# Output projection: a second set of accumulators in idle PSUM tiles, partial sums stored from ScalarE's queue, t3 loaded in place

## The chip, the cores and the metric

The kernel runs on one core of one Trainium2 chip. The metric is the device time of one execution in microseconds (us); less is better.

## The reference

A two-layer backbone works on 1024 latent tokens of 1024 channels, in float32. The first layer is a convolution branch beside a gated linear recurrence, the second a pooling mixer. What matters here is the end of the second layer, its output projection, the gated residual and the final norm:

```python
def odd_mixer(h, p, on_grid):
    ...
    y = jnp.einsum("bngi,gij->bngj", d, p["w_grp"]).reshape(bn, n, W_POOL) * p["scale"]
    return (y * jax.nn.silu(g)) @ p["w_out"]      # (1024 x 2048) @ (2048 x 1024)
...
        x = x + gate[:, None] * out_x
    return rmsnorm(x, final_g)
```

## The kernel before

Channels lie on the 128 partitions and tokens along the free dimension, so the projection has a weight of 2048 x 1024, an input `y` of 16 tiles of 128 x 1024 and an output of 8 such tiles. The 2048 input channels are taken in two **parts** of 1024. Part 0's result, times the gate and added to `x`, goes to DRAM (`x1_part`); part 1 reads it back (`x2_load`), adds its own, and the final norm follows.

**Blocks.** Within a part the output is made in four blocks: block `m` (0, 2, 4, 6) is the output tiles `m` and `m+1`, each in two halves of 512 tokens. A block is a two-by-two matrix product done with seven half-size products instead of eight. The seven operands made from `y` are named `b11, t1, t2, b21, t3, b22, t4`; the weights have seven matching combinations, here weight 1 to weight 7. Each operand and each weight is split into a high half of reduced precision (`fp32r`, by a cast on ScalarE, ACT) and a low half (the rest, by a subtraction on VectorE, DVE; both in `split`, lines 97 to 99). A product (`prod`, lines 1148 to 1157) runs over four steps of 128 input channels with three matmuls each: high x high (L1152), high weight x low operand (L1154), low weight x high operand (L1155). So it is 12 matmuls of 128 x 512, and its third matmul is the first that needs the weight's low half.

**Accumulators.** A block uses three PSUM tiles of one bank, `a`, `c` and `b`. `a` takes b11, is copied by ACT into `b` (`evac`), and goes on with b21; `c` takes t1 and b22; `b` takes t2, t3 and t4 on top of the copy. In between, `put` takes partial values out: `keep_part` copies one with ACT (L1209), `copied` does so for the second half (L1836), L1898 adds them on DVE, and `gated` (L1828) multiplies by the gate and adds the sum to a tile `xp` that has been loaded from `x1_part` (L1892) and is then stored there (L1901). The three PSUM tiles come from the pool `pm`, which has four buffers, so a block's tiles are those that the block before has just used. The other four banks are the tiles `c0` and `c1` (one bank each) and the two-bank tile `xb` of the pool `pc`; in this stage they are idle until the final norm.

**Order on PE.** The matmuls of the projection are chained by hand (`linked`). For part 0, block `m` runs b11 and t1, then t4 of the block before (`pend`, `last`), then t2, b21, and t3 and b22 in the order given. Blocks 0 and 2 of part 1 are written out with the class `Quad`; blocks 4 and 6 follow in `last_half0` and in the tail.

**Weights.** `wquad_steps` loads the two raw tiles of a block (`wr`, two buffers, L1116) on SyncE's (SP's) DMA queue and makes the seven weights from them. L1132 is `s3`, from which weight 7 is made; L1133 makes the raw of weight 5, L1134 that of weight 6, L1141 that of weight 3. The order of making is 1, 5, 6, 2, 7, 3, 4. The next block's raw tiles can be loaded when the last split of this block has read them.

**Operands.** The operands of `y` have been stored in DRAM (`y_raw`); `y_operand` loads an operand in two halves (L1703) and splits each. With `raw_tile` given, the load goes into a tile of its own; without, it goes "in place" into the tile that later holds the low half. `y_sums` (L1096 to L1100) makes t1 to t4 for two tiles of `y`; for the last two tiles it is called in the middle of part 0's block 2. Its tile `yt` is a `vtile`, of which there are two buffers; they are shared with every second `xp` tile. The `xp` tiles take turns between `vtile` and `atile`, two buffers each.

**Order on the other engines.** It is planned when the kernel is built, from the priorities, the dependences and modelled times. `issue_after` (and `held`) keeps an instruction behind another, and `high_priority` lets the `put`s and copies go ahead. Each engine, SP's queue among them, then runs its list in order: an instruction that waits holds those behind it.

Of the kernel before, what the change touches and what calls it, by code (L numbers as in the profile page):

```python
# [20 lines left out]
KT = D // P  # L21
H = 512
HALF = (slice(0, H), slice(H, S))
# [24 lines left out]
BOPS = ("b11", "t1", "t2", "b21", "t3", "b22", "t4")  # L48
# [3 lines left out]
def body(ctx, tc, xT, ctxT, cc, ccol, modT, modW, win, gw, wout, wu, grp, wg, wo1, small, edge, ident, outT):  # L52
    nc = tc.nc
# [15 lines left out]
    x1_part = [dram.tile([P, S], F32, tag=f"x1_part{j}", name=f"x1_part{j}") for j in range(KT)]  # L69
# [13 lines left out]
    def psum(name):  # L83
        return pm.tile([P, H], F32, tag="mm", name=name)


    def wide(name):
        return pc.tile([P, S], F32, tag="xb", name=name)


    def banks(name, n):
        if n % 2:
            t = wide(name)
            return [t[:, h] for h in HALF]
        return [pc.tile([P, H], F32, tag=f"c{i}", name=f"{name}_{i}") for i in range(2)]

    def split(src, hi, lo, eng):
        return (nc.scalar.copy(hi, src),  # L98
                eng.tensor_tensor(out=lo, in0=src, in1=hi.bitcast(F32), op=sub))

    def held(after):
        return tc.issue_after(after.ins) if after is not None else nullcontext()

    def split_held(src, hi, lo, eng, low):
        nc.scalar.copy(hi, src)
        with held(low):
            eng.tensor_tensor(out=lo, in0=src, in1=hi.bitcast(F32), op=sub)

    class Written:

        def __init__(self, eng):
            self.eng, self.last = eng, None
# [184 lines left out]
    with ExitStack() as sctx:  # L297
# [335 lines left out]
        for i in range(2):  # L633
            v = cx[i].rearrange("p (k n) -> p k n", n=C)
# [185 lines left out]
    with ExitStack() as actx:  # L820
# [79 lines left out]
        w = w_vg0  # L900
# [202 lines left out]
    loaded, parted, subbed = [None], [], [None]  # L1103


    def wquad(*args, **kw):
        ops = {}
        for _ in wquad_steps(ops, *args, **kw):
            pass
        return tuple(ops[n] for n in range(1, 8))  # L1110

    def wquad_steps(ops, src, name, ring, late=False, hold=None):
# [98 lines left out]
    kept_ = [None]  # L1211
# [483 lines left out]
    def y_operand(ops, part, name, raw_tile, alloc, later=None, hold=None):  # L1695
        hi, lo = [], []
        for q in range(2):
            if raw_tile is None:
                lo.append(alloc(f"y{part}_{name}l{q}", F32R))
                r = lo[q].bitcast(F32)  # L1700
            else:
                r = raw_tile(f"yr_{part}_{name}_{q}")
            d = nc.sync.dma_start(r, y_raw[part][name][:, q * S : (q + 1) * S])  # L1703
            if name in ("b22", "t4"):
                y_loaded[name == "t4"] = d
            hi.append(alloc(f"y{part}_{name}h{q}", F32R))
            if raw_tile is not None:
                lo.append(alloc(f"y{part}_{name}l{q}", F32R))
            if later is not None:
                later.append((r, hi[q], lo[q]))  # L1710
            else:
                with held(hold):
                    split(r, hi[q], lo[q], nc.vector)
        halves = lambda ts: [t[:, h] for t in ts for h in HALF]
        ops[name] = halves(hi), halves(lo)
# [3 lines left out]
    def y_operands(part, raws, names=BOPS, alloc=None, later=None, hold=None):  # L1719
        for name in names:  # L1720
            y_operand(yops[part], part, name, next(raws),
                      alloc or (dtile if name in ("b11", "b21", "t4") else d2tile), later, hold)
# [8 lines left out]
            return wpool.tile([P, D], F32R, tag=tag, name=name)  # L1731
        return ring

    def wo1_weights(part, m):
        return wquad([wo1[m + i, part] for i in range(2)], f"wo{part}_{m}", wo1_ring,
                     part == 1 and m >= KT - 4)

    wo1_ring = wo_ring(iter(["x", "x", "x", "wh", "wl", "wh", "wl"] + ["wh", "wl", "d", "d"] * 14))
    vps, silu = [], [None]
# [94 lines left out]
    def copied(name, x):  # L1834
        t = ttile(f"b_{name}")
        copied_[0] = nc.scalar.copy(t, x)  # L1836
        return t

    copied_ = [None]

    chain = [None]

# [2 lines left out]
            chain[0] = prod(*args)  # L1845
        return chain[0]

    def quad_linked(w, name, ops, put, ahead, order, pend):
        p1, p2, p3, p4, p5, p6, p7 = w
        a, c, b = psum(f"qa_{name}"), psum(f"qc_{name}"), psum(f"qb_{name}")  # L1850
        linked(a, p1, ops["b11"], True, False)
        with tc.high_priority(offset=EVAC):
            evac = nc.scalar.copy(b, a)
        linked(c, p5, ops["t1"], True, False)
        with tc.high_priority(offset=EVAC):
            put(1, 1, c, 0)
        if pend is not None:
            pend()
        linked(b, p6, ops["t2"], False, False)
        with tc.high_priority(offset=EVAC):  # L1860
            put(0, 1, b, 0)
        linked(a, p2, ops["b21"], False, True)
        with tc.high_priority(offset=EVAC):
            put(0, 0, a, None)
        with tc.issue_after(evac.ins):
            nxt_ = ahead()
        for name in order:
            if name == "t3":
                linked(b, p7, ops["t3"], False, False)
                with tc.high_priority(offset=EVAC):  # L1870
                    put(1, 1, b, 1)
            else:
                linked(c, p3, ops["b22"], False, True)
                with tc.high_priority(offset=EVAC):
                    put(0, 1, c, 1)

        def last():
            linked(b, p4, ops["t4"], False, True)
            with tc.high_priority(offset=EVAC):
                put(1, 0, b, None)  # L1880
        return nxt_, last

    last_ = None
    for m in range(0, KT, 2):

        def put(i, h, x, part, m=m, parts={}):
            if part == 0:
                keep_part(parts, f"wo0_{m}", i, x)
                return
            xp_n[0] += 1  # L1890
            t = (vtile, lambda name: atile(name)[:, :H])[xp_n[0] % 2](f"xp{m}_{i}_{h}")
            nc.sync.dma_start(t, x1_part[m + i][:, HALF[h]])  # L1892
            if part == 1:

                if i == 1:
                    x = copied(f"wo0_{m}", x)
                s = x if i == 0 else parts[i]
                nc.vector.tensor_tensor(out=s, in0=x, in1=parts[i], op=add)  # L1898
                x = s
            gated(m + i, t, x)  # L1900
            nc.sync.dma_start(x1_part[m + i][:, HALF[h]], t)  # L1901
            if (m, i, h, part) == (2, 1, 1, 1):
                y_sums(NK - 2)
        def nxt(m=m):
            if m == 0:
                with tc.issue_after(kept_[0].ins):
                    for v in y_late:
                        split(*v, nc.vector)
            if m < KT - 2:
                with tc.issue_after(stored[0].ins):  # L1910
                    return wo1_weights(0, m + 2)
            w = wo1_weights(1, 0)
            y_operands(1, iter([xtile]), BOPS[3:4])
            return w

        if m == KT - 2:
            with tc.issue_after(loaded[0].ins):
                y_operands(1, iter([xtile] * 2), BOPS[1:3])
        w, last_ = quad_linked(w, f"wo0_{m}", yops[0], put, nxt, ("b22", "t3") if m else ("t3", "b22"), last_)
        if m == 2:  # L1920
            with tc.issue_after(loaded[0].ins):
                y_operands(1, iter([xtile]), BOPS[:1], lambda name, dt: xtile(name, dt), hold=copied_[0])
# [8 lines left out]
    def wo1_put(m):  # L1931
        def put(i, h, x, part):
            v = x1[m + i][:, HALF[h]]
            if i == 1 and part == 1:
                x = copied(f"wo1_{m}", x)
            gated(m + i, v, x)
            if part != 0:
                square_fin(m + i, h, slice(0, H), v)
        return put

    class Quad:

        def __init__(self, w, name, put):
            self.w, self.name, self.put = dict(zip(range(1, 8), w)), name, put
            self.ps = {}

        def bank(self, n):
            if n not in self.ps:
                self.ps[n] = psum(f"q{n}_{self.name}")
            return self.ps[n]  # L1950

        def run(self, op):
# [12 lines left out]
            with tc.high_priority(offset=EVAC):  # L1965
                self.evac = nc.scalar.copy(self.bank("b"), self.bank("a"))

    q0 = Quad(w, "wo1_0", wo1_put(0))
    for n in "acb":
        q0.bank(n)  # L1970
    q0.run("b11")
    q0.copy()
    q0.run("t1")
    last_()
    q0.run("t2")
    q0.run("b21")
    with tc.issue_after(q0.evac.ins):
        late_ = []
        y_operands(1, iter([None]), BOPS[5:6])
        y_operands(1, iter([xtile]), BOPS[4:5])  # L1980
        with held(y_loaded[0]):
            y_operands(1, iter([None]), BOPS[6:], later=late_)
        w = wo1_weights(1, 2)
        for v in late_:
            split(*v, nc.vector)
        with held(y_loaded[1]):
            x2_load(2)
    q2 = Quad(w, "wo1_2", wo1_put(2))
    q2.run("b11")
    q0.run("t3")  # L1990
    q0.run("b22")
# [300 lines left out]
```

## Time and profile before

| | us |
|---|---|
| median of three runs | 1278.67 |
| lowest and highest of them | 1275.99, 1279.72 |
| the profiled execution | 1275.34 |
| its span (first to last instruction) | 1273.5 |
| its granted TensorE clock, mean | 0.995 |

A row of a timeline gives the start, the length in us, the engine, the line of the kernel, the operation, the tiles (output <- inputs, buffer numbers left out), and in square brackets how long the engine stood idle before it and what ended that. Rows of neighbouring equal instructions are merged (x2, x3). A row of waits gives who waited, for whom, the total in us, how often, and the longest. `wq_wo` are the split weights of this projection, `wr_wo` the raw ones, `y_t4l` is the low half of operand t4 and `y_t4h` its high half, `qa_wo`, `qb_wo` and `qc_wo` are the accumulators, `b_wo` and `s_wo` the copies out of them. `wo0_2` is block 2 of part 0, `wo1_0` block 0 of part 1.

### The profile page before, as it was taken

The numbers are of one execution on the slowest core, as the hardware profiler recorded it, in microseconds if no ns is written. First come the engines' busy times: TensorE is split into PE (matmuls) and PEld (weight loads), VectorE is DVE, ScalarE is ACT, GpSimd is POOL, SyncE is SP. The second block draws the span as 40 slices with busy tenths as digits, with TensorE's granted clock in tenths as the row PEclk, the third lists the DMA queues.
The fourth block names the chain that finished last, engine by engine and source line by source line (L and its number), as shares of the span: only waits on it lengthen the run. The fifth ranks groups of instructions, "written<-read, shape, count | busy, mean of one in ns | idle before, by whom it ended". The sixth has DMA issues, their size and how long they took to land. (4 is left out here: it accounts for less than half of the span.)

```text
span 1273.5 us, 16213 instructions
## 1 busy us (share of the span) xinstructions
PE 1254.7 (99%) x5858; PEld 1036.0 (81%) x5858; DVE 1139.2 (89%) x1748; ACT 655.9 (51%) x955; POOL 295.0 (23%) x176
## 2 busy tenths in 40 slices
PE   9999999999999999999999999999999999999996
PEld 7788888888888888888887888888888888777785
DVE  7799999999999999989888979999999977878876
ACT  8464566556656533237444446644444444735542
POOL 0015364436443557434210032000000000000003
PEclk9999999999999999999999999999999999999998
DMA  9970111112111234432526665334333235868713
GB/s 375 380 254 33 58 59 58 50 47 70 59 66 58 75 116 142 157 131 83 175 90 232 201 225 159 105 139 157 124 116 100 107 116 182 279 193 268 284 67 133
DMA packets 78705, 182.29 MB, mean 143 GB/s; under 512 B 7712, under 2 KB 23328, under 8 KB 78624
## 3 DMA queue, kind: packets, MB, share of 16 engines
q1 hardware_dynamic: 69632, 176.53, 40.7%
q10 hardware_dynamic: 8992, 4.72, 1.3%
q8 instruction: 46, 0.75, 0.3%
q14 instruction: 35, 0.29, 0.1%
HBM read 137.18 MB, written 44.04 MB: 142 GB/s over the span
## 5 line engine op out<-in xcount | busy, mean ns | idle before, releaser
L670 DVE SCALAR_TENSOR_TENSOR conv<-u,sm,conv 128x505 f32<-128x505 f32 (+6 forms) x224 | 153.8, 747 | 1.0
L2012 POOL TENSOR_TENSOR o<-x,rr 128x256 f32<-128x256 f32 (+1 forms) x10 | 9.8, 1012 | 455.6 <-ACT rr L2012 455.6
L670 ACT ACTIVATE l<-g,sm 128x512 f32<-128x512 f32 (+1 forms) x96 | 58.7, 619 | 57.7 <-PE g L670 57.0
L670 POOL TENSOR_TENSOR l<-l,l 128x1280 f32<-128x1280 f32 x16 | 47.1, 2966 | 25.6 <-ACT l L670 15.1
L670 PE MATMUL gb<-h0h,wl_gb 128*128 128x512 f32 x128 | 49.9, 390 | 0.4 <-POOL wl_gb L670 0.4
L670 PE MATMUL va<-h0h,wl_va 128*128 128x512 f32 x128 | 49.9, 390 | 0.2 <-DVE wl_va L670 0.2
L670 PE MATMUL gb<-h0h,wh_gb 128*128 128x512 f32 x128 | 49.9, 389 | 0.0
L670 PE MATMUL gb<-h0l,wh_gb 128*128 128x512 f32 x128 | 49.8, 389 | 0.0
L670 PE MATMUL va<-h0l,wh_va 128*128 128x512 f32 x128 | 49.8, 389 | 0.0
L670 PE MATMUL va<-h0h,wh_va 128*128 128x512 f32 x128 | 49.8, 389 | 0.0
L670 PE MATMUL wob<-ybh,wh_wob 128*128 128x512 f32 x128 | 49.8, 389 | 0.0
L670 PE MATMUL wob<-ybl,wh_wob 128*128 128x512 f32 x128 | 49.8, 389 | 0.0
L670 PE MATMUL wob<-ybh,wl_wob 128*128 128x512 f32 x128 | 49.8, 389 | 0.0
L670 DVE TENSOR_TENSOR_SCAN l<-l,l 128x256 f32<-128x256 f32 (+1 forms) x32 | 48.7, 1521 | 1.1
L670 DVE SCALAR_TENSOR_TENSOR conv<-cL,wsum,conv 128x506 f32<-128x506 f32 (+3 forms) x70 | 48.2, 746 | 0.2
L670 POOL TENSOR_TENSOR l<-l,uc 128x1280 f32<-128x1280 f32 x16 | 47.7, 3008 | 0.0
L98 ACT CAST wq_g<-wr_g 128x512 fp32r<-128x512 f32 x48 | 28.2, 620 | 31.7 <-DMA wr_g<-wg 12.2
L670 PE MATMUL xb<-h0l,wh_xb 128*128 128x512 f32 x112 | 43.8, 391 | 0.0
L670 PE MATMUL xb<-h0h,wh_xb 128*128 128x512 f32 x112 | 43.8, 391 | 0.0
L670 PE MATMUL xb<-h0h,wl_xb 128*128 128x512 f32 x112 | 43.6, 389 | 0.0
L670 PE MATMUL vg<-h0h,wh_vg 128*128 128x512 f32 x112 | 43.6, 389 | 0.0
L670 PE MATMUL vg<-h0l,wh_vg 128*128 128x512 f32 x112 | 43.6, 389 | 0.0
(624 smaller groups left out, 4312.4 us busy)
## 6 DMA issues: line engine op xcount, KB each, us to landing
modw<-modW SPq DMA_DIRECT2D x16, 512.0 KB, 10.7
x_part<-xp SPq DMA_DIRECT2D x32, 256.0 KB, 2.4
mod<-modT SPq DMA_DIRECT2D x32, 256.0 KB, 3.7
wr_v<-wfold SPq DMA_DIRECT2D x16, 512.0 KB, 3.9
wr_g<-wg SPq DMA_DIRECT2D x16, 512.0 KB, 4.4
wr_wo<-wo SPq DMA_DIRECT2D x16, 512.0 KB, 4.6
mod<-modT SPq DMA_DIRECT2D x14, 512.0 KB, 4.2
yr_t<-y_t SPq DMA_DIRECT2D x14, 512.0 KB, 6.5
```

The lines of the kernel that those rows point to most:

```text
L98: return (nc.scalar.copy(hi, src), eng.tensor_tensor(out=lo, in0=src, in1=hi.bitcast(F32), op=sub))
L670: last[eng] = f(*args, **kw)
L2012: tail[eng] = f(*args, **kw)
```

## The change

1. In part 0, blocks 2 and 6 (`m % 4 == 2`) take `a` and `c` from the tiles `c0` and `c1` and `b` from the second half of `xb` (`spare`). Block 2 of part 1 (`q2`) does so too. The other blocks stay in `pm`.
2. The stores of part 0's sums to `x1_part` are no longer issued on SP right behind `gated`. They are kept in a list (`kept_out`) and issued on ACT's DMA queue (`stores`), held behind a later copy: behind `copied` of the same block (all but the newest when it isn't the first block), behind the `keep_part` copy of t1 of the next block, and at the end behind the copy `q0.evac` of part 1's first block.
3. In part 0's block 0, the splits of t4 are taken out of the list that runs ahead of the next block's weights; they are issued after weight 5, through the new argument `mid` of `wquad`, and their subtractions are held behind weight 5's low half.
4. In part 1, t3 is loaded in place and first; the raw weights of block 2 are held behind its second load; b22 and t4 are loaded in place behind those raw weights, and both are split behind the weights' splits. Before, the order was b22 (in place), t3 (through a tile of its own), t4 (in place), weights.

```diff
-    def wquad(*args, **kw):
+    def wquad(*args, mid=None, **kw):
         ops = {}
         for _ in wquad_steps(ops, *args, **kw):
-            pass
+            if mid is not None:
+                mid()
         return tuple(ops[n] for n in range(1, 8))
...
-            if name in ("b22", "t4"):
+            if name in ("t3", "t4"):
                 y_loaded[name == "t4"] = d
...
-    copied_ = [None]
+    copied_, kept_out = [None], []
+
+    def stores(after, n):
+        with held(after):
+            for _ in range(n):
+                nc.scalar.dma_start(*kept_out.pop(0))
...
+    def spare(name):
+        a, c = banks(f"qac_{name}", 0)
+        return a, c, wide(f"qb_{name}")[:, HALF[1]]
+
-    def quad_linked(w, name, ops, put, ahead, order, pend):
+    def quad_linked(w, name, ops, put, ahead, order, pend, other):
         p1, p2, p3, p4, p5, p6, p7 = w
-        a, c, b = psum(f"qa_{name}"), psum(f"qc_{name}"), psum(f"qb_{name}")
+        a, c, b = spare(name) if other else [psum(f"q{n}_{name}") for n in "acb"]
...
         with tc.high_priority(offset=EVAC):
             put(1, 1, c, 0)
+            stores(kept_[0], len(kept_out))
         if pend is not None:
             pend()
...
+    def second_late():
+        with tc.issue_after(kept_[0].ins):
+            for v in y_late[2:]:
+                split_held(*v, nc.vector, parted[1])
...
                 if i == 1:
                     x = copied(f"wo0_{m}", x)
+                    stores(copied_[0], len(kept_out) - (m > 0))
...
             gated(m + i, t, x)
-            nc.sync.dma_start(x1_part[m + i][:, HALF[h]], t)
+            kept_out.append((x1_part[m + i][:, HALF[h]], t))
...
             if m == 0:
                 with tc.issue_after(kept_[0].ins):
-                    for v in y_late:
+                    for v in y_late[:2]:
                         split(*v, nc.vector)
+                with tc.issue_after(stored[0].ins):
+                    return wo1_weights(0, 2, second_late)
...
-        w, last_ = quad_linked(w, f"wo0_{m}", yops[0], put, nxt, ("b22", "t3") if m else ("t3", "b22"), last_)
+        w, last_ = quad_linked(w, f"wo0_{m}", yops[0], put, nxt, ("b22", "t3") if m else ("t3", "b22"), last_,
+                               m % 4 == 2)
...
     q0.run("t1")
+    stores(q0.evac, 2)
     last_()
     q0.run("t2")
+    stores(q0.evac, 1)
     q0.run("b21")
     with tc.issue_after(q0.evac.ins):
         late_ = []
-        y_operands(1, iter([None]), BOPS[5:6])
-        y_operands(1, iter([xtile]), BOPS[4:5])
+        y_operands(1, iter([None]), BOPS[4:5])
         with held(y_loaded[0]):
-            y_operands(1, iter([None]), BOPS[6:], later=late_)
-        w = wo1_weights(1, 2)
+            w = wo1_weights(1, 2)
+        with tc.issue_after(loaded[0].ins):
+            y_operands(1, iter([None] * 2), BOPS[5:], later=late_)
         for v in late_:
             split(*v, nc.vector)
         with held(y_loaded[1]):
             x2_load(2)
-    q2 = Quad(w, "wo1_2", wo1_put(2))
+    q2 = Quad(w, "wo1_2", wo1_put(2), spare("wo1_2"))
```

More of the change, by code (lines that the diff above doesn't have):

```diff
@@ L1732, in wo_ring, with wo1_weights @@
         return ring
-    def wo1_weights(part, m):
+    def wo1_weights(part, m, mid=None):
         return wquad([wo1[m + i, part] for i in range(2)], f"wo{part}_{m}", wo1_ring,
-                     part == 1 and m >= KT - 4)
+                     part == 1 and m >= KT - 4, mid=mid)
     wo1_ring = wo_ring(iter(["x", "x", "x", "wh", "wl", "wh", "wl"] + ["wh", "wl", "d", "d"] * 14))
@@ L1941, in body, with __init__ @@
     class Quad:
-        def __init__(self, w, name, put):
-            self.w, self.name, self.put = dict(zip(range(1, 8), w)), name, put
-            self.ps = {}
+        def __init__(self, w, name, put, tiles):
+            self.w, self.put = dict(zip(range(1, 8), w)), put
+            self.ps = dict(zip("acb", tiles))
         def bank(self, n):
-            if n not in self.ps:
-                self.ps[n] = psum(f"q{n}_{self.name}")
             return self.ps[n]
@@ L1966, in copy @@
                 self.evac = nc.scalar.copy(self.bank("b"), self.bank("a"))
-    q0 = Quad(w, "wo1_0", wo1_put(0))
-    for n in "acb":
-        q0.bank(n)
+    q0 = Quad(w, "wo1_0", wo1_put(0), [psum(f"q{n}_wo1_0") for n in "acb"])
     q0.run("b11")
```

## The prediction

> **What bounds the kernel now.** I read the page's busy times first, then the waits of PE behind 900 us, then the busy times by stretch, then PE's timeline, and last the timelines of DVE, ACT and SP around each hole.
>
> ```profile
> PE 1254.7 (99%) x5858; PEld 1036.0 (81%) x5858; DVE 1139.2 (89%) x1748; ACT 655.9 (51%) x955; POOL 295.0 (23%) x176
> ```
> ```profile
> PE qc_wo L1152 <- DVE xp L1828: 2.8, 2, 1.8
> PE qa_wo L1155 <- DVE wq_wo L99: 1.9, 2, 1.2
> ...
> PE qa_wo L1152 <- ACT wq_wo L98: 0.4, 1, 0.4
> ...
> PE qb_wo L1154 <- DVE y_t3l L99: 0.2, 1, 0.2
> ```
> ```profile
> 1093.50:1217.00 123.50, 118.14 (x506) 95.10 (x505) 99.74 (x141) 65.58 (x101) 0.00 (x0) 0.99 0.70 236
> 1110.00:1130.00 20.00, 16.93 (x66) 12.97 (x66) 12.04 (x19) 6.16 (x12) 0.00 (x0) 0.91 0.38 126
> ...
> 1170.00:1190.00 20.00, 20.00 (x89) 16.33 (x87) 15.61 (x23) 8.26 (x13) 0.00 (x0) 1.00 0.88 312
> ```
>
> PE is the bound, and the stage that the diff touches, 1093.5 to 1217 us, still has holes in it. Columns of the last view are start:end, length, PE, PEld, DVE, ACT, POOL, granted clock, DMA share, GB/s. DVE is busy 99.74 of 123.5 us there: a shorter stage leaves it less slack.
>
> ```profile
> 1093.51 0.39 PE L1152 MATMUL qa_wo<-y_b11h,wq_wo 128*128 128x512 f32 x1
> ...
> 1109.83 0.39 PE L1152 MATMUL qc_wo<-y_b22h,wq_wo 128*128 128x512 f32 x1
> ...
> 1114.46 0.50 PE L1155 MATMUL qa_wo<-y_b11h,wq_wo 128*128 128x512 f32 x1 [1.25 <-DVE wq_wo L99]
> ...
> 1118.88 0.47 PE L1152 MATMUL qc_wo<-y_t1h,wq_wo 128*128 128x512 f32 x1 [1.82 <-DVE xp L1828]
> 1119.19 0.40 PE L1154 MATMUL qc_wo<-y_t1l,wq_wo 128*128 128x512 f32 x1
> 1119.43 0.46 PE L1155 MATMUL qc_wo<-y_t1h,wq_wo 128*128 128x512 f32 x1
> ...
> 1120.33 0.63 PE L1155 MATMUL qc_wo<-y_t1h,wq_wo 128*128 128x512 f32 x1
> ...
> 1123.32 0.45 PE L1152 MATMUL qb_wo<-y_t4h,wq_wo 128*128 128x512 f32 x1
> ...
> 1159.91 0.47 PE L1152 MATMUL qc_wo<-y_t1h,wq_wo 128*128 128x512 f32 x1 [0.95 <-DVE xp L1828]
> ...
> 1190.49 0.50 PE L1152 MATMUL qa_wo<-y_b11h,wq_wo 128*128 128x512 f32 x1 [0.38 <-ACT wq_wo L98]
> ...
> 1191.84 0.50 PE L1155 MATMUL qa_wo<-y_b11h,wq_wo 128*128 128x512 f32 x1 [0.61 <-DVE wq_wo L99]
> ...
> 1194.83 0.50 PE L1154 MATMUL qb_wo<-y_t3l,wq_wo 128*128 128x512 f32 x1 [0.21 <-DVE y_t3l L99]
> ...
> 1216.94 0.39 PE L1152 MATMUL qa_l<-y_b11h,wq_wo 128*128 128x512 f32 x1
> ```
>
> The first two rows are six products of 12 matmuls apart: 16.32 us over 72, a cadence of 0.2267 us. The first and the last row are 42 products apart (one left over from before, four blocks of seven, wo1_0's seven, six of wo1_2's): 504 matmuls, 114.2 us at that cadence, against 123.4 measured. So 9.2 us are lost in the stage, and that is the ceiling of the gain. The six named waits are 5.2 of it. Between 1120.33 and 1123.32 seven starts take 2.99 us instead of 1.59: 1.4 us at a low clock (granted 0.91 over that stretch). The other 2.6 us are restarts, about 0.3 us behind each wait (first matmuls of 0.50 instead of 0.39), and crumbs.
>
> **Part by part.** *The two bank waits (1118.88 and 1159.91).* Both wait for a `gated` of the block before on its c accumulator. With wo0_2, wo0_6 and wo1_2 in the other three tiles, neither bank has a reader when it is wanted. At 1159.91 nothing else is late, so 0.95 plus a restart goes: 1.2 us. At 1118.88 something is just behind it:
>
> ```profile
> 1111.97 0.69 DVE L1132 TENSOR_TENSOR ws_wo<-wr_wo,wr_wo 128x512 f32<-128x512 f32 x1 [0.81 <-DMA wr_wo<-wo]
> 1112.58 1.22 DVE L99 TENSOR_TENSOR y_t4l<-yr_t,y_t4h 128x1024 fp32r<-128x1024 f32 x1
> 1113.72 0.68 DVE L99 TENSOR_TENSOR wq_wo<-wr_wo,wq_wo 128x512 fp32r<-128x512 f32 x1
> ...
> 1114.92 0.68 DVE L1133 TENSOR_TENSOR wr_wo<-wr_wo 128x512 f32<-128x512 f32 x1
> ...
> 1117.99 0.75 DVE L1828 SCALAR_TENSOR_TENSOR xp<-qc_wo,m,xp 128x512 f32<-128x512 f32 x1
> 1118.65 1.89 DVE L99 TENSOR_TENSOR wq_wo<-wr_wo,wq_wo 128x512 fp32r<-128x512 f32 x3
> ```
> ```profile
> 1115.64 0.62 ACT L98 CAST wq_wo<-wr_wo 128x512 fp32r<-128x512 f32 x1 [2.20 <-DVE wr_wo L1133]
> ```
>
> The bank came free at 1118.74; the low half of weight 5, first of the three in 1.89 us from 1118.65, was ready about 1119.3, and the third matmul of t1 (1119.43) needs it. With the bank free and nothing else changed PE would stop two matmuls later. The edit `second_late` matters here: it takes the y_t4l subtraction (1112.58) from ahead of weight 1's low half and holds it behind weight 5's. Everything after it moves up 1.14 us, the distance of the two starts.
>
> *Weight 1 (1114.46).* Its low half then starts at 1112.58 and ends near 1113.25; the third matmul was due at 1113.0. Left 0.3 and a restart: 1.0 of 1.5 saved.
>
> *Weight 5.* Due near 1116.0 then. In today's order it would be ready about 1118.2, 2.1 us late. L1133 no longer stands behind y_t4l; right behind weight 1's low half, or one or two `gated` operations later, it starts at 1113.2 to 1114.4, and cast and subtraction (0.62, 0.69) put weight 5 at 1115.3 to 1116.5. I take 0.5 late and a restart: 1.5 of 2.3 saved. y_t4l's two subtractions (2.4 us) then run from 1116.5 to 1118.9; t4's product comes two products and the two rests of waiting behind b11's 1112.6, near 1119.4, so they are covered with half a microsecond to spare. Without that cover they would cost what they overrun.
>
> *The clock.* The 1.4 us follow two waits of 1.25 and 1.82 us within 6 us; the waits of 0.95, and of 0.38, 0.61 and 0.21 together, are followed by none. With waits of 0.3 and 0.5 I count it gone: 1.4 saved, bounds 0 and 1.4. The Trainium skill (TensorE: Matmul & The Clock Gate, Part 1) has the clock halve after at least one idle window of about 3.4 us; no hole here is that long, so by that rule these waits did not cause the drop, it would stay, and the sum would be 1.4 smaller. The trace speaks for a finer trigger; it is a rival below.
>
> *t3 in place, weights earlier (wo1_2).*
>
> ```profile
> 1188.87 1.05 ACT L98 CAST y_b22h<-y_b22l 128x1024 fp32r<-128x1024 f32 x1 [4.30 <-DMA y_b22l<-y_b]
> 1189.83 1.13 ACT L98 CAST wq_wo<-wr_wo 128x512 fp32r<-128x512 f32 x2
> ```
> ```profile
> 1177.75 1.54 SPq L1116 DMA_DIRECT2D wr_wo<-wo  x2
> ```
>
> ACT stood 4.30 us at the cast of y_b22h, with weight 1's cast behind it although its rows had come: the subtraction of L1132, which needs both raw tiles, ran at 1187.65. The diff sends t3 first, then the weights, then b22 and t4, whose splits come behind the weights'. The blocking cast goes, and t3, needed by the next product, is there: 0.9 us (0.21, an unnamed second hole at its other half, two restarts). Its first load goes into tiles that wo0_6's t3 product reads, as b22's second load (1179) did, so SP stands until that product is done, and the weights' loads stand behind it. And 1 MB of t3 now stands ahead of the weights on SP where 0.5 MB of b22 stood, on DMA engines 0.88 busy at 312 GB/s: 0.5 MB is 1.6 us. So of 1.5 us (0.38, 0.61, two restarts) I save 1.0.
>
> *The stores.*
>
> ```profile
> L1901 SPq DMA_DIRECT2D x_part<-xp x16: 319/320/628, 1110.1 to 1189.0; - x16
> ...
> DMA to landing us min/median/max: 2.0/4.1/9.4
> ```
> ```profile
> L285 ACTq DMA_DIRECT2D wfold<-fo x16: 366/366/385, 750.1 to 795.0; - x16
> ```
>
> Sixteen issues leave SP (5.1 us) and cost ACT 5.9 us at 0.366; ACT is busy 65.58 of 123.5 us, so I cost them at nothing, with SP's loads freed from waiting behind a `gated`. Uncovered, each would be 0.4. They add waits on ACT: each stands there until its `gated` has run on DVE, and the casts and the copies b<-a that PE wants stand behind it. By the order of the calls the sums stored behind a copy are those of the products before it, already gated when the copy runs; the exceptions are the last two groups, behind q0's copy, where ACT stood idle for 4.30 us in the row above. Bounds 0 and 2 us, taken 0. The Trainium skill (DMA: Bandwidth & Descriptors, Issuing engines are not separate DMA queues) says that issuing from several engines saves only sequencer time; by that rule too the bytes gain nothing. What the holding-back costs is tiles, the slower rival.
>
> *Sum.* 1.2 + 1.0 + 1.5 + 1.4 + 0.9 + 1.0 = 7.0. PE then asks 4 to 6 us sooner for raws that go round by DMA and DVE; bounds 0 and 3, from the 0.88 DMA share and DVE's 24 us of slack; I take 1.0. Gain 6.0 us: the profiled execution goes from 1275.34 (span 1273.5 and 1.84 around it) to 1269.3. The median of the runs, 1278.67, lies 3.33 above it: **1272.7**.
>
> **Rivals.**
> *Weight 5 takes the bank's place.* The planner keeps DVE's order of today; t1 stops 2.1 us and the clock drops again. Weight 5's 1.5 and the 1.4 are not saved: gain 3.1, 1275.6. For it: the 1118.65 row; against: program order puts weight 5 ahead of weights 6, 2 and 7.
> *The low clock stays.* Gain 4.6, 1274.1.
> *DVE stands at a held-back tile (slower).*
>
> ```profile
> 1129.82 0.70 DVE L1096 TENSOR_TENSOR yt<-y,y 128x512 f32<-128x512 f32 x1 [2.77 <-DMA x_part<-xp]
> ```
> ```profile
> 1139.94 0.57 ACT L1836 COPY b_wo<-qb_wo 128x512 f32<-128x512 f32 x1
> ```
>
> The tile of `yt` is that of wo0_0's last sum, and DVE waited 2.77 us for its store already. That store now goes behind the copy of wo0_2 (1139.94): 0.57 + 0.37 + 9.4 at the longest landing is 1150.3, and the four sums end near 1152.8. If they stand ahead of weight 6's low half, wanted by t2's product at 1145.2, PE stops 7.6 us, with a restart and, for a hole over twice as long, twice the clock's 1.4: 10.7 lost against 6.0 saved, 1283.4. It turns to a loss if landing passes about 5 us and the planner puts the sums ahead. Against it: the median landing is 4.1, and DVE may take the sums later.
> *It does nothing:* the waits return at other weights, 1278.7.
>
> **How the numbers follow.** A measurement here can tell about 0.3% (3.8 us; the three runs span 3.7). Forecast 0.48, weight 5 0.22, DVE stands 0.17, clock stays 0.08, nothing 0.05. Faster by over 0.3% (under 1274.8): 0.48 + 0.06 + 0.06 of weight 5 = 0.60; same 0.23 (0.16 of weight 5, the rest from nothing and the edges); slower 0.17. Range: full removal of 9.2 with a fast set of runs, 1268.5 (0.03 below), up to 1280.5, which leaves out the stand of DVE. The likeliest case alone: 1269.5 to 1274.7.
>
> **What would show it.** Right: no PE wait on `xp` L1828 in this stage, no row near 0.63 us, granted clock 1.00 in the stretch behind 1110, under 3.5 us lost of 114.2. Weight 5: a wait of t1 on DVE `wq_wo`. DVE stands: a long idle before L1096, PE waiting on `wq_wo` in wo0_4. I am wrong if the stage is not shorter than 120 us, or if the loss returns behind 1217 us.

## The result, and the profile after

The median fell from 1276.84 us (six runs, 1275.99 to 1279.72; the 1278.67 of the start were the first three such runs) to **1269.06 us** (six runs, 1267.5 to 1270.9): a ratio of 0.9935 [0.992, 0.995], 7.8 us between the medians. The profiled executions stand at 1275.34 and 1268.66, their spans at 1273.5 and 1266.9. Lines of the kernel behind 1106 have moved: the raw loads, L1116, are L1117 now, L1152, L1154 and L1155 of before are L1153, L1155 and L1156 now, L1132 to L1134 are L1133 to L1135, L1828 is L1829, and the stores, L1901 on SP before, are L1845 on ACT.

The page's busy times, PE's waits in the stage, and the same stretches as before (start:end, length, PE, PEld, DVE, ACT, POOL, granted clock, DMA share, GB/s), of the changed kernel:

```profile
PE 1251.0 (99%) x5858; PEld 1034.7 (82%) x5858; DVE 1140.9 (90%) x1748; ACT 655.1 (52%) x955; POOL 295.0 (23%) x176
```
```profile
PE qac_wo L1156 <- DVE wq_wo L99: 1.2, 2, 0.8
...
PE qc_wo L1155 <- DVE y_b22l L99: 0.4, 1, 0.4
PE qac_wo L1153 <- ACT wq_wo L98: 0.3, 1, 0.3
```
```profile
1093.00:1210.50 117.50, 115.52 (x506) 94.32 (x506) 99.20 (x141) 65.18 (x101) 0.00 (x0) 1.00 0.70 248
...
1110.00:1130.00 20.00, 19.23 (x86) 15.59 (x85) 13.89 (x20) 7.66 (x13) 0.00 (x0) 1.00 0.47 154
...
1170.00:1190.00 20.00, 20.00 (x89) 16.54 (x89) 19.96 (x29) 11.96 (x17) 0.00 (x0) 1.00 0.94 345
```

The same 506 matmuls and 141 DVE instructions stand in 117.5 us instead of 123.5. The 20 us behind 1110 hold 86 matmuls where there were 66, at a granted clock of 1.00 instead of 0.91. PE's waits sum to 1.9 us where they were 5.2, and none is on `xp`, that is, on a bank. PE's timeline, shortened to the ends of the stage and all of its waits, says where they are:

```profile
1093.04 0.39 PE L1153 MATMUL qa_wo<-y_b11h,wq_wo 128*128 128x512 f32 x1
...
1116.22 0.50 PE L1156 MATMUL qac_wo<-y_t1h,wq_wo 128*128 128x512 f32 x1 [0.77 <-DVE wq_wo L99]
...
1154.43 0.50 PE L1153 MATMUL qac_wo<-y_t1h,wq_wo 128*128 128x512 f32 x1 [0.29 <-ACT wq_wo L98]
...
1155.64 0.50 PE L1156 MATMUL qac_wo<-y_t1h,wq_wo 128*128 128x512 f32 x1 [0.48 <-DVE wq_wo L99]
...
1192.87 0.50 PE L1155 MATMUL qc_wo<-y_b22l,wq_wo 128*128 128x512 f32 x1 [0.44 <-DVE y_b22l L99]
...
1210.46 0.39 PE L1153 MATMUL qa_l<-y_b11h,wq_wo 128*128 128x512 f32 x1
```

From first to last row 117.42 us; against 114.2 for the 504 matmuls 3.2 are lost, where 9.2 were. So the stage gives 6.0; it also starts 0.47 sooner (1093.04 against 1093.51) and ends 6.48 sooner, and the span is 6.6 shorter, so nothing comes back behind it. "Loss" below is always this number, taken the same way in the profiled execution of each kernel.

### The profile page after: what moved, and what is told of

Its sections match the earlier page's. It is cut to its first block, busy times and chain, and to the rows that moved or that the text cites. A ratio compares the mean times of both kernels' runs of the same rounds, so it can differ in the third digit from the quotient of the medians.

```text
span 1266.9 us, 16191 instructions
## 1 busy us (share of the span) xinstructions
PE 1251.0 (99%) x5858; PEld 1034.7 (82%) x5858; DVE 1140.9 (90%) x1748; ACT 655.1 (52%) x955; POOL 295.0 (23%) x176
## 5 line engine op out<-in xcount | busy, mean ns | idle before, releaser
L98 ACT CAST wq_wo<-wr_wo 128x512 fp32r<-128x512 f32 x48 | 28.6, 619 | 41.9 <-DMA wr_wo<-wo 20.9
L98 ACT CAST wq_v<-wr_v 128x512 fp32r<-128x512 f32 x48 | 28.2, 620 | 34.4 <-DMA wr_v<-wfold 15.9
L99 DVE TENSOR_TENSOR wq_wo<-wr_wo,wq_wo 128x512 fp32r<-128x512 f32 x48 | 32.0, 686 | 13.7 <-ACT wq_wo L98 13.6
## 6 DMA issues: line engine op xcount, KB each, us to landing
modw<-modW SPq DMA_DIRECT2D x16, 512.0 KB, 10.2
```

The lines of the kernel that those rows point to most:

```text
L98: return (nc.scalar.copy(hi, src), eng.tensor_tensor(out=lo, in0=src, in1=hi.bitcast(F32), op=sub))
```

## The experiments

Three theories stood at the start. A: each part removes its own waits, and the parts lean on each other where two waits stand one behind the other. B: the banks carry nearly all of the gain. C: the stores' leaving SP carries what the banks don't. The table gives each kernel's ratio to the kernel before on the same chip, that ratio in us of 1276.8, and the loss of its profiled execution.

| kernel | what it is | ratio [95%] | us | loss |
|---|---|---|---|---|
| before | | 1 | 0 | 9.2 |
| after | | 0.9935 [0.992, 0.995] | -8.3 | 3.2 |
| e1_banks | before + spare banks | 0.9994 [0.9986, 1.0003] | -0.8 | 10.5 |
| e2_t4_late | before + t4 behind weight 5 | 1.0013 [1.0, 1.0025] | +1.7 | 11.1 |
| e3_banks_t4 | before + both | 0.9971 [0.996, 0.9981] | -3.7 | 6.2 |
| e4_order | before + wo1_2's order | 0.9984 [0.9973, 0.9994] | -2.0 | 7.3 |
| e5_stores_sp | after, stores on SP again | 0.9944 [0.9928, 0.996] | -7.1 | 2.8 |
| e6_no_banks | after without the banks | 0.9985 [0.9974, 0.9996] | -1.9 | 7.7 |
| e7_old_order | after, wo1_2's old order | 1.0007 [0.9996, 1.0018] | +0.9 | 10.2 |
| n4_all | after + three cures | 0.9946 [0.993, 0.9962] | -6.9 | 2.8 |
| n1_w6 | after + one of them | 0.9936 [0.9923, 0.9949] | -8.2 | 1.6 |
| n5_w6_sp | n1_w6, stores on SP | 0.9942 [0.9928, 0.9955] | -7.4 | 4.0 |

### The banks alone

```diff
+    def spare(name):
+        a, c = banks(f"qac_{name}", 0)
+        return a, c, wide(f"qb_{name}")[:, HALF[1]]
...
+        a, c, b = spare(name) if other else [psum(f"q{n}_{name}") for n in "acb"]
...
     q2 = Quad(w, "wo1_2", wo1_put(2))
+    q2.ps = dict(zip("acb", spare("wo1_2")))
```

> The kernel before, with the spare accumulators alone. Theory A (the prediction's): weight 5 stands right behind the bank, so in wo0_2 the wait at t1 only moves two matmuls on and the rows near 0.63 us stay; wo0_6's wait (1.2 us with its restart) goes. Stage loss from 9.2 to between 7.4 and 8.0 us, 1.2 to 1.8 us faster than before. Rival B (the banks carry the gain): the wait, its restart, the low clock and wo0_6's wait all go, 4.9 us faster. Rival C (SP freed of the stores carries the gain): no change over 1.2 us.

Measured: 0.9994, nothing that can be told from no change. Its PE timeline, in wo0_2 and in wo1_2:

```profile
1119.11 0.50 PE L1155 MATMUL qac_wo<-y_t1h,wq_wo 128*128 128x512 f32 x1 [1.89 <-DVE wq_wo L99]
...
1121.04 0.63 PE L1152 MATMUL qac_wo<-y_t1h,wq_wo 128*128 128x512 f32 x1
...
1191.41 0.50 PE L1152 MATMUL qac_wo<-y_b11h,wq_wo 128*128 128x512 f32 x1 [2.84 <-ACT wq_wo L98]
```

Before, t1's first matmul waited 1.82 us for the bank and started at 1118.88. With the bank free t1's third waits 1.89 for weight 5's low half and starts at 1119.11: the wait moved two matmuls on, as the prediction had it, the rows at 0.63 still behind it. The wait of wo0_6 is gone, but PE then comes to wo1_2 1.5 us sooner than before (1188.57 against 1190.11, the start less the wait), finds weight 1 ready 0.9 later (1191.41), and waits 2.84 instead of 0.38. B falls. What A had not was that the second bank's gain would be given back too.

### t4 behind weight 5 alone

```diff
-                    for v in y_late:
+                    for v in y_late[:2]:
                         split(*v, nc.vector)
+                with tc.issue_after(stored[0].ins):
+                    return wo1_weights(0, 2, second_late)
```

> The kernel before, with t4's splits behind weight 5 alone. Theory A: weight 1's wait shrinks by 1.0 us and DVE's list moves up 1.1 us, so the bank comes free 1.1 us sooner and PE comes 1.0 us sooner: a wait of about 1.7 us at t1 stays. 1.0 us faster, or 2.4 if the low clock goes with the shorter first wait. Rival B: 1.0 us. Rival C: nothing over 1.0.

A miss: 1.0013, rather slower. Rows of PE, then of DVE:

```profile
1118.75 0.76 PE L1153 MATMUL qc_wo<-y_t1h,wq_wo 128*128 128x512 f32 x1 [3.37 <-DVE xp L1829]
1119.31 0.63 PE L1155 MATMUL qc_wo<-y_t1l,wq_wo 128*128 128x512 f32 x1
```
```profile
1116.12 1.21 DVE L107 TENSOR_TENSOR y_t4l<-yr_t,y_t4h 128x1024 fp32r<-128x1024 f32 x1
...
1117.86 0.74 DVE L1829 SCALAR_TENSOR_TENSOR xp<-qc_wo,m,xp 128x512 f32<-128x512 f32 x1
```

Weight 1's wait is gone as expected. But the subtraction of y_t4l that was taken from ahead of weight 1 now stands ahead of the `gated` that frees the bank. It runs at 1117.86, as it did before (1117.99), PE comes to it earlier, and so the two waits of 1.25 and 1.82 have become one of 3.37.

### Both

The edits of the two kernels above together:

```diff
+        a, c, b = spare(name) if other else [psum(f"q{n}_{name}") for n in "acb"]
...
+                    return wo1_weights(0, 2, second_late)
```

> The kernel before, with the spare accumulators and t4's splits behind weight 5; stores on SP and wo1_2's loads as before. Theory A: the two together are worth more than their sum, because the bank and weight 5 ended the same wait: 1.0 + 1.5 + 1.4 + 1.2 = 5.1 us faster, and no row near 0.63 us. Rival B: 5.9, the sum of the two alone (4.9 and 1.0). Rival C: under 2.5, since SP still holds the stores.

Measured 3.7 us, under the 5.1 of A, under the 5.9 of B, over the 2.5 that C allowed. Apart the two give -0.8 and +1.7, together -3.7: in wo0_2 only a wait of 0.57 is left. What is left of the loss stands in wo1_2, PE above, ACT below:

```profile
1185.96 0.50 PE L1153 MATMUL qac_wo<-y_b11h,wq_wo 128*128 128x512 f32 x1 [2.48 <-ACT wq_wo L98]
...
1187.89 0.63 PE L1153 MATMUL qac_wo<-y_b11h,wq_wo 128*128 128x512 f32 x1
```
```profile
1184.34 1.04 ACT L98 CAST y_b22h<-y_b22l 128x1024 fp32r<-128x1024 f32 x1 [4.07 <-DMA y_b22l<-y_b]
1185.29 1.14 ACT L98 CAST wq_wo<-wr_wo 128x512 fp32r<-128x512 f32 x2
```

That is the blocking cast of the prediction: ACT stands 4.07 us at y_b22h with weight 1's cast behind it. PE comes to this weight at 1183.48 (the start less the wait), 6.6 us sooner than before's 1190.11; the weight is ready 4.5 sooner; so 0.38 of waiting have become 2.48.

### wo1_2's order alone

```diff
-            if name in ("b22", "t4"):
+            if name in ("t3", "t4"):
...
-        y_operands(1, iter([None]), BOPS[5:6])
-        y_operands(1, iter([xtile]), BOPS[4:5])
+        y_operands(1, iter([None]), BOPS[4:5])
         with held(y_loaded[0]):
-            y_operands(1, iter([None]), BOPS[6:], later=late_)
-        w = wo1_weights(1, 2)
+            w = wo1_weights(1, 2)
+        with tc.issue_after(loaded[0].ins):
+            y_operands(1, iter([None] * 2), BOPS[5:], later=late_)
```

> The kernel before, with wo1_2's loads in the new order alone (t3 in place and first, weights, b22, t4). Theory A: the waits at 1190.49, 1191.84 and 1194.83 go but for some 0.5 us: 1.9 us faster, the first 100 us of the stage unchanged. Rival D (the DMA engines are the limit there): the weights land as late behind t3's 1 MB as behind b22's, under 0.5 us faster.

The amount came as expected, 2.0 us. Its place did only in part, as PE's waits in wo0_2 and wo1_2 show (wo0_6 keeps its wait for the bank):

```profile
1114.35 0.50 PE L1155 MATMUL qa_wo<-y_b11h,wq_wo 128*128 128x512 f32 x1 [1.19 <-DVE wq_wo L99]
...
1118.77 0.47 PE L1152 MATMUL qc_wo<-y_t1h,wq_wo 128*128 128x512 f32 x1 [1.86 <-DVE xp L1828]
...
1189.12 0.47 PE L1152 MATMUL qa_wo<-y_b11h,wq_wo 128*128 128x512 f32 x1 [0.43 <-DVE xp L1828]
1190.23 0.51 PE L1155 MATMUL qa_wo<-y_b11h,wq_wo 128*128 128x512 f32 x1 [0.40 <-DVE wq_wo L99]
```

wo1_2 still waits, now for a bank as well: from wo1_0's b21 product on, 2.0 us are lost in this profile and 2.5 in that of before, so the half microsecond explains a quarter of the 2.0. The rest of the smaller loss is a low clock that did not come, though the two waits of wo0_2 are nearly as long as before's and nothing was edited there. It is not this one execution alone: the mean granted clock of all twelve runs is 0.996 at the median, that of before on the same chip 0.995. How the edit of wo1_2 could bring that is not shown; the last section takes it up. So the amount was met, but in this profile three quarters of it have another place than was expected.

### The whole without the stores on ACT

```diff
-            stores(kept_[0], len(kept_out))
...
-                    stores(copied_[0], len(kept_out) - (m > 0))
...
-            kept_out.append((x1_part[m + i][:, HALF[h]], t))
+            nc.sync.dma_start(x1_part[m + i][:, HALF[h]], t)
...
-    stores(q0.evac, 2)
...
-    stores(q0.evac, 1)
```

> The kernel after, with the stores back on SP right behind each sum. Theory A (the stores are worth nothing by themselves): within 1 us of the kernel after. Rival C (loads behind the stores on SP decide when weights come): waits for weights return in wo0_6 or wo1_2, 2 to 4 us slower than the kernel after.

0.9944 [0.9928, 0.996] against 0.9935 [0.992, 0.995]: with the stores on SP 7.1 of the 8.3 us are still there, so C, by which the stores carry what the banks don't, falls. What their move is worth beside the rest, 1.2 us here, is smaller than the intervals; these alone leave room for some 4. A wait of 1.09 for weight 1's low half is back in wo1_2 (1186.83), as C had it, but wo0_6 has no wait at all, and the stage loses 2.8 instead of 3.2. In the changed kernel the stores and the waits for their landing, and then the same waits with the stores on SP:

```profile
L1845 ACTq DMA_DIRECT2D x_part<-xp x16: 326/327/592, 1110.7 to 1184.3; - x16
```
```profile
SPq L1908 <- DMA x_part<-xp: 42.3, 9, 9.2
```
```profile
SPq L1907 <- DMA x_part<-xp: 21.2, 10, 5.5
...
SPq L1916 <- DVE xp L1829: 23.9, 9, 5.7
```

Off SP the stores no longer wait there for `gated` (23.9 us), but SP's loads wait for stores that leave later (42.3 instead of 21.2): the sum is the same 42 to 45 us. The rule of the Trainium skill that the prediction cited (DMA: Bandwidth & Descriptors, Issuing engines are not separate DMA queues) says that issuing from several engines saves only the sequencer's time. This pair of runs agrees as far as it can tell: another issuing engine brought nothing clear of the intervals. With wo1_2's old order it is another matter, see below.

### The whole without the banks

```diff
-        a, c, b = spare(name) if other else [psum(f"q{n}_{name}") for n in "acb"]
+        a, c, b = [psum(f"q{n}_{name}") for n in "acb"]
...
-    q2 = Quad(w, "wo1_2", wo1_put(2), spare("wo1_2"))
+    q2 = Quad(w, "wo1_2", wo1_put(2), [psum(f"q{n}_wo1_2") for n in "acb"])
```

> The kernel after, with all accumulators back in the four buffers of pm. Theory E (each part only unmasks the next limit, so all are needed): t1 of wo0_2 waits 3.4 us for its bank as with t4 late alone, wo0_6's bank wait of about 1 us is back, 4 to 6 us slower than the kernel after. A theory in which the parts add up independently: 1.2 us for wo0_6 and about 1.5 for wo0_2, under 3 us slower.

1274.87 us, 5.0 above the 1269.92 of the kernel with stores on SP, which ran on the same chip. Against the changed kernel itself, by the ratios, it is 6.4. That is about the 4 to 6 expected, from an edit that alone gave 0.8. Its PE timeline has the bank's wait back, longer than before's 1.82:

```profile
1119.86 0.77 PE L1153 MATMUL qc_wo<-y_t1h,wq_wo 128*128 128x512 f32 x1 [3.07 <-DVE xp L1829]
```

The bank wait expected in wo0_6 did not come back; t1 waits there 0.41 for weight 5 (1161.01), and b22 in wo1_2 1.08 for its low half (1199.12).

### The whole with wo1_2's old order

```diff
-            if name in ("t3", "t4"):
+            if name in ("b22", "t4"):
...
-        y_operands(1, iter([None]), BOPS[4:5])
+        y_operands(1, iter([None]), BOPS[5:6])
+        y_operands(1, iter([xtile]), BOPS[4:5])
         with held(y_loaded[0]):
-            w = wo1_weights(1, 2)
-        with tc.issue_after(loaded[0].ins):
-            y_operands(1, iter([None] * 2), BOPS[5:], later=late_)
+            y_operands(1, iter([None]), BOPS[6:], later=late_)
+        w = wo1_weights(1, 2)
```

> The kernel after, with wo1_2's loads and splits in the old order. Theory E: PE reaches wo1_2 some 5 us sooner than in the kernel before and finds its first weight behind y_b22h's cast on ACT, as with banks and t4 late: waits of about 2.5 and 0.6 us, perhaps the low clock, 3 to 5 us slower than the kernel after. If the parts add up independently: 1.9 us slower, what the order alone took off the kernel before.

1278.09 us: 8.2 above the 1269.92, where 3 to 5 were expected. The direction was right, the size was not, and the wait expected at weight 1 did not come: PE waits for t3. PE's rows, then ACT's, then ACT's of the banks with t4 late (`e3_banks_t4`):

```profile
1190.70 0.50 PE L1155 MATMUL qb_wo<-y_t3l,wq_wo 128*128 128x512 f32 x1 [0.94 <-DVE y_t3l L99]
...
1194.17 0.79 PE L1153 MATMUL qb_wo<-y_t3h,wq_wo 128*128 128x512 f32 x1 [2.04 <-ACT y_t3h L98]
...
1197.78 0.79 PE L1155 MATMUL qb_wo<-y_t3l,wq_wo 128*128 128x512 f32 x1 [2.81 <-DVE y_t3l L99]
```
```profile
1190.66 2.00 ACT L98 CAST y_t4h<-y_t4l 128x1024 fp32r<-128x1024 f32 x2
...
1193.07 1.05 ACT L98 CAST y_t3h<-yr_t 128x1024 fp32r<-128x1024 f32 x1
```
```profile
1189.41 1.04 ACT L98 CAST y_t3h<-yr_t 128x1024 fp32r<-128x1024 f32 x1 [1.47 <-DMA yr_t<-y_t]
...
1192.45 2.00 ACT L98 CAST y_t4h<-y_t4l 128x1024 fp32r<-128x1024 f32 x2
```

Here t4's two casts stand ahead of t3's second, though t3 is wanted first; in the kernel with the banks and t4 late they stand behind it. This kernel waits 5.8 us for t3 where that one waited 2.5 and 0.61 for weight 1. The two have the same banks, t4's splits and old order, and differ in the stores alone: on SP there, on ACT here. So beside the old order the stores' move costs 4.6 us, from -3.7 to +0.9, with intervals that do not meet (0.9971 [0.996, 0.9981] and 1.0007 [0.9996, 1.0018]). With the stores on SP the order is worth 3.4 us, from -3.7 to -7.1; the rest of the 8.2 is what the stores cost without it. By which step the stores change the planner's list is not shown.

### What is left: three cures, and one of them

Three things were seen late in the changed kernel. Weight 6's combination (L1135) runs ahead of weight 5's low half. wo0_6's raw weights come late. And y_b22l is late in wo1_2. `n4_all` puts weight 6's combination behind weight 5's low half, gives all kept stores to the first later copy, and raises the splits of b22. `n1_w6` does the first alone, and `n5_w6_sp` does it with the stores on SP. The comments in the lines below are not in the kernels.

```diff
+        if w6_held and not late:
+            ops[5] = op(a21, 5)
+            with held(parted[1]):
+                nc.vector.tensor_tensor(out=a11, in0=a21, in1=a11, op=sub)
...
-                    stores(copied_[0], len(kept_out) - (m > 0))
+                    stores(copied_[0], len(kept_out))            # n4_all alone
...
-    stores(q0.evac, 2)
+    stores(q0.evac, len(kept_out))                               # n4_all alone
...
+        for v in late_[:2]:                                      # n4_all alone
+            with tc.high_priority(offset=EVAC):
+                split(*v, nc.vector)
```

> The kernel after with three more edits, one for each of its remaining holes (1.04, 1.32 and 0.71 us): weight 6's combination held behind weight 5's low half; every kept store issued at the first copy behind it; b22's splits in wo1_2 at the priority of the evacuations. Theory A (these holes are DVE's order and SP's wait for a tile): 1 to 2 us faster than the kernel after. Theory E: each hole that closes lets PE run into the next late weight, under 1 us.

> The kernel after with weight 6's combination held behind weight 5's low half, and nothing else. Theory A: the holes at weight 5 in wo0_2 (1.04 us) and wo0_6 (1.32) shrink by 0.6 each, one DVE operation: 1.2 us faster than the kernel after. Theory E: PE then waits in wo1_2, within 0.6 us of the kernel after.

> The same edit with the stores back on SP. Theory A: the stores on SP cost nothing, so within 0.6 us of the kernel with weight 6 held and the stores on ACT; wo0_2's hole (0.46 us with the stores on SP) goes.

`n4_all` is no better than the change (0.9946): its PE waits 0.6 for weight 1's low half, 0.6 for the copy `b_wo` and 0.5 for `s_wo`, none of which the changed kernel has; that the raised splits and stores took the places of others is likely, but not shown by a run that leaves one of them out. `n1_w6` closes the holes it aims at, as DVE's rows and the only two waits that its PE has left show:

```profile
1115.00 0.68 DVE L99 TENSOR_TENSOR wq_wo<-wr_wo,wq_wo 128x512 fp32r<-128x512 f32 x1
1115.60 0.69 DVE L1138 TENSOR_TENSOR wr_wo<-wr_wo,wr_wo 128x512 f32<-128x512 f32 x1
```
```profile
1093.93 0.50 PE L1162 MATMUL qa_wo<-y_b11h,wq_wo 128*128 128x512 f32 x1 [0.18 <-DVE wq_wo L99]
...
1154.14 0.51 PE L1159 MATMUL qac_wo<-y_t1h,wq_wo 128*128 128x512 f32 x1 [0.20 <-ACT wq_wo L98]
```

Weight 5's wait in wo0_2 is gone, and of the three of 0.77, 0.29 and 0.48 one of 0.20 is left; in the profile the loss is 1.6 instead of 3.2. The ratio, 0.9936, is the change's own 0.9935, so the 1.2 us that it was expected to gain over the change are not shown by the times. With the stores on SP it is no better either (0.9942): 0.8 us behind `n1_w6` where 0.6 were allowed, within the intervals, and wo0_2's hole, which was to go, is a wait of 0.48 (1117.38). No kernel here beat the change by more than can be measured.

### The kernel before, once more

> The kernel before once more, for its low clock. If its waits at weight 1 and at t1 in wo0_2 (1.25 and 1.82 us) decide it, some seven starts at twice the distance follow them again, 1.4 us. If it depends on more than the waits (the kernel with the new order alone showed the same two waits and no low clock), it may be missing.

One execution, 1274.57 us, span 1272.8. PE's two waits in wo0_2, and a row behind them:

```profile
1115.07 0.50 PE L1155 MATMUL qa_wo<-y_b11h,wq_wo 128*128 128x512 f32 x1 [0.61 <-DVE wq_wo L99]
...
1119.49 0.47 PE L1152 MATMUL qc_wo<-y_t1h,wq_wo 128*128 128x512 f32 x1 [1.86 <-DVE xp L1828]
...
1121.03 0.39 PE L1152 MATMUL qc_wo<-y_t1h,wq_wo 128*128 128x512 f32 x1
```

The bank's wait is 1.86, nearly as it was, and the row 1.5 us later is 0.39 long: no low clock. But weight 1's wait is only half as long (0.61, before 1.25), so this run does not part its two expectations; the kernel with the new order alone, with 1.19 and 1.86, is the closer test. The loss of this execution is 8.0 instead of 9.2. So the clock's term is not in every execution of the same kernel.

## Why the prediction was right

It said 1272.7, in 1268.5 to 1280.5, and most likely faster by over 0.3%; it is 1269.06, faster by 0.65% [0.5, 0.8]. Against the profiled execution it was closer: 6.0 forecast for the stage and 6.0 found. Of the 3.6 us between 1272.7 and 1269.06, 1.83 are the median of before, which went from 1278.67 to 1276.84 with three more runs. The rest is the 7.8 between medians against 6.0, which lies just under the ratio's interval (6.4 to 10.2 us). Adding a full 3.33 us from a profile to a median that rested on three runs was the weak step; in the changed kernel the median lies only 0.40 above the profiled execution. All four signs named for being right came. So did the sign of the rival *weight 5*, a wait of t1 on `wq_wo`, but at 0.77 us instead of 2.1. That the stage's 6.0 were met to the tenth is luck: terms below were off by up to 1.0 us, and the misses cancel.

**The bank waits** (1.2 in wo0_6): right as to the banks. At 1154.43 and 1155.64, in the same t1, PE now waits 0.29 and 0.48 for weight 5, with two restarts 1.3 in all, as much as the 1.2 that had been saved. This is the larger part of the pay-back, forecast at 1.0 without a place. The changed kernel's rows of SP, then of ACT, then of DVE, show how it comes:

```profile
1143.14 0.32 SPq L1908 DMA_DIRECT2D xp<-x_part  x1
...
1143.99 0.42 SPq L1117 DMA_DIRECT2D wr_wo<-wo  x1
...
1145.41 0.33 SPq L1117 DMA_DIRECT2D wr_wo<-wo  x1
```
```profile
1149.95 1.14 ACT L98 CAST wq_wo<-wr_wo 128x512 fp32r<-128x512 f32 x2 [6.00 <-DMA wr_wo<-wo]
```
```profile
1151.83 0.69 DVE L1133 TENSOR_TENSOR ws_wo<-wr_wo,wr_wo 128x512 f32<-128x512 f32 x1
```

Both raw loads leave SP late. ACT stands 6.00 us for the first, from which weight 1 is made; L1133 on DVE, with weight 5's raw behind it, needs both. With the stores on SP the raws left at 1141.28 and 1142.95, and L1133 ran at 1148.34. In the changed kernel SP's list stood 1.9 us for one of `y_sums`' results (before 1139.09), 1.7 for the landing of the store of `yt` (before 1141.19) and 0.8 for that of a held-back store (before 1143.14). DVE makes these sums late: `yt` at 1136.04, with the stores on SP at 1125.60. With the stores on SP wo0_6 has no wait at all, so step 2 of the change takes here what step 1 gives.

**Weight 1** (1.0 of 1.5): under-sized, it went wholly. **Weight 5** (ready 1115.3 to 1116.5, 0.5 late): right. DVE of the changed kernel:

```profile
1111.20 0.69 DVE L99 TENSOR_TENSOR wq_wo<-wr_wo,wq_wo 128x512 fp32r<-128x512 f32 x1 [2.15 <-ACT wq_wo L98]
...
1114.28 0.69 DVE L1135 TENSOR_TENSOR wr_wo<-wr_wo,wr_wo 128x512 f32<-128x512 f32 x1
...
1115.48 0.68 DVE L99 TENSOR_TENSOR wq_wo<-wr_wo,wq_wo 128x512 fp32r<-128x512 f32 x1
1116.08 1.22 DVE L107 TENSOR_TENSOR y_t4l<-yr_t,y_t4h 128x1024 fp32r<-128x1024 f32 x1
```

The low half ends at 1116.16, and PE waits 0.77 for it, 1.04 with the restart (0.8 forecast). L1135, which weight 5 does not need, stands ahead of it; it is what `n1_w6` moved. y_t4l's subtraction follows at once and delays nobody.

**The clock** (1.4): right in the profiled execution, but over-read. The new order alone has nearly the same two waits (1.19 and 1.86) and no drop, and the repeated run of before, with 0.61 and 1.86, has none either. So waits of that length do not decide it alone, which one profile cannot show, and that the profile of before had the drop is luck for this term.

**wo1_2** (0.9 for t3, 1.0 for the weights): both waits went, the weights' with all of its 1.5. y_b22l, split behind the weights as the diff has it, now costs 0.44 and a restart at 1192.87, 0.7 in all. With wo0_6's 1.3 the pay-back is 2.0, forecast at 1.0.

**The stores at nothing**: not refuted beside the new order, as the kernel with stores on SP shows; the issue cost is 0.327 at the median, not 0.366. Beside the old order their move costs 4.6 us, so the term is nothing only because the order changes with it, which the prediction did not say.

**The slower rival** did not come as it was drawn. One row of DVE decides:

```profile
1136.04 0.68 DVE L1096 TENSOR_TENSOR yt<-y,y 128x512 f32<-128x512 f32 x1
```

DVE takes `yt` 6.2 us later than before (1129.82), behind what weights 5 and 6 need, and does not stand idle for its tile at all. The price of taking it later is the one in wo0_6 above.

What the prediction did not see, though its sum survived it, is that the terms are not a sum. The banks alone gave -0.8, t4 alone +1.7, the order alone -2.0: -1.1 together, against -7.1 for these three in one kernel (the stores on SP) and -8.3 with the stores moved. Two pairs carry this. Banks and t4 together give -3.7, 4.6 more than apart. The stores and the order are the other pair: the stores' move costs 4.6 beside the old order and nothing that can be measured beside the new one. So of the 8.2 that go with the order only 3.4 are its own, which the intervals do not part from the 2.0 that it brought alone. Taken away from the whole the banks cost 5.0; how much of that is again the stores on ACT stays open, since no run leaves the banks out with the stores on SP. The prediction wrote that PE "would stop two matmuls later" in wo0_2; the same holds from block to block, since PE that comes 6.6 us sooner to wo1_2 meets weights that were only just in time.

## What to carry to other kernels

A wait in a profile hides the next one, often two instructions or one block behind it. So price an edit by what is late next, and try edits that unmask one another together: parts that bring nothing or a loss alone may be most of the gain together. It holds the other way too: a part that is worth nothing beside one order (the stores) may cost several microseconds beside another. Where a busy engine is freed, look for what is moved into the freed place, since y_t4l, moved from ahead of a weight, went ahead of a bank's release and gave all of it back. A term that one profiled execution shows once, like a clock drop, is priced with a chance until a second execution shows it again.

## What the runs showed of the hardware

Not expected was how short a stand of PE goes with matmuls at a low clock: rows 0.63 us long, about 0.43 apart instead of 0.2267, for 2.7 to 5.7 us. Every PE wait of over 2.0 us that the profiles of this stage have is among them. Behind waits of 3.37 (t4 late) and 3.07 (no banks) the first matmul is already slow (0.76 and 0.77 long). Behind 2.84 (banks) and 2.48 (banks with t4 late) the slow rows start 1.3 us on, behind a second wait of 0.61. In the old order 2.04 is followed by one slow matmul (0.79) and at once by 2.81 with more of them. A low clock also followed pairs of 1.25 and 1.82 (before) and of 1.02 and 1.89 (banks), some 4 us apart, but not pairs of 1.19 and 1.86 (order alone) or of 0.61 and 1.86 (before once more). Over all runs the mean granted clock of the kernel before spreads from 0.993 to 0.997 (0.995 in 33 of 68 runs, 0.997 in 8), at mean spans of 1278.2 us for 0.993 and 1273.6 for 0.997. The changed kernel has 0.996 or 0.997 in all six, the one with the old order 0.992 to 0.994 in all twelve.

The Trainium skill (TensorE: Matmul & The Clock Gate, Part 1) lets the clock halve after at least one idle window of about 3.4 us, in a window that runs freely. All of these waits are shorter than that, though 3.37 comes near, and those of the pairs are about half of it, so as a least length of one wait it doesn't hold here; a window that runs freely would fit that the same waits go either way, but no run here shows the window itself. What the trigger is stays open. The prediction's low-clock rival, built on that rule, did not come, but neither do the runs show that the waits it removed caused every drop.
